# One offset for all tiles, half a projection moved to the last stage, and two pairs of banks swapped, in a two-layer encoder on one core

## The chip, the cores and the metric

The kernel runs on one core of a Trainium2 chip. The metric is the device time of one execution in microseconds (us); lower is better. TensorE (PE in the profile) multiplies, ScalarE (ACT) and VectorE (DVE) split, scale and add, SyncE (SP) issues the DMAs, GpSimd (POOL) does almost nothing.

## The reference

Two token sequences, 512 and 256 long, go through the same two layers with shared weights and a model width of 1024. Cut to what matters:

```python
for i in range(2):                      # layer 0: attention, layer 1: short convolution
    h = rms_norm(x, norm_mix[i])
    x = x + (window_attention(h, ...) if i == 0 else short_conv(h, ...))
    h = rms_norm(x, norm_mlp[i])
    x = x + square(relu(h @ mlp_w_up[i])) @ mlp_w_down[i]          # 1024 -> 4096 -> 1024
    gate = sigmoid(rms_norm(x, norm_ple[i]) @ ple_w_gate[i])
    x = x + (p[i] @ ple_w_proj[i]) * gate                          # p[i]: 256 inputs per token
return rms_norm(x, final_norm)
```

`p[i] @ ple_w_proj[i]`, the projected inputs, does not depend on x and can be made at any time.

## The kernel before, in words

**Precision.** Every float32 operand of a product is split in two parts of type fp32r: `hi`, a rounded copy that ACT makes, and `lo`, the rest, which DVE makes as operand minus `hi`. A product is then three matmuls: hi·hi, hi·lo, lo·hi.

**Stages.** The trace runs through: attention with its projections (0 to about 270 us); the first MLP (270 to 750), the gate with the projected inputs (750 to 860), the convolution mixer (860 to 1100), the second MLP (1100 to 1545), and the last stage (1545 to the end), which finishes the second MLP, makes the second gate and the final norm and stores both outputs. In the MLPs and the mixer most products go through a scheme with seven block products in place of eight: `seven_parts` and `down`, whose matmuls all stand on line 464 (`product7`). One such chunk is 84 matmuls of 384 columns: seven products of 12, into PSUM tiles named a, b, c, d (for `down`: a, b, B, C). Before a chunk's products, ACT and DVE form sums of weight blocks (`sum`) and split them into the weight tiles whi/wlo, zhi/zlo and vhi/vlo.

**Order.** In attention and in the last stage the instructions are first recorded as operations with a cost each and then laid out by a list scheduler (`Plan.order`); elsewhere the order is that of the code. Each engine works its own queue in that order.

**Places.** SBUF tiles come from pools, which are laid behind each other: `const`, `main` (x), `slots` (S0 to S31: activations and their parts), `wp` (raw weights and whi/wlo), `stat`, and then, for attention, `attn` and `tmpA`, and afterwards `more` (S32 and up, zhi/zlo, vhi/vlo, `sum`) and `tmpB`. Most tiles are a multiple of 512 bytes long in each partition, but a few are not: the tiles `z` and `y` of the mixer (771 floats in four of the places S), `fin` (16 floats in `stat`), and in `attn` the tiles rb, rc, mn, sm and L. Each of these shifts what is laid behind it. As built, byte addresses modulo 512 are: x 96; the places S 96, 128, 160, 192 and, for most, 224; whi/wlo and the raw weights 224; everything in `more` and `tmpB` 288; `attn` mostly 160, `tmpA` 160. A matmul therefore reads its weights (whi/wlo) at 224 or (zhi/zlo, vhi/vlo) at 288, and its moving operand at any of the six.

**Projected inputs of layer 1.** They are made early and kept in DRAM (`pj`, `pjt`) until the last stage loads them (tile `pr`). For the second sequence (256 tokens, two blocks of 128, kept with the tokens in the partitions) the first 512 of the 1024 features are made in attention (`second_projected`, line 1237, 12 matmuls of 512 columns) and the other 512 at the head of the first MLP (`second_inputs.product`, line 1388, called from `ahead`), together with half of the first sequence's.

**The head of the first MLP.** `ahead` makes six products, each in a PSUM bank of the pools A (4 banks), C (2) and B (2): `bank("AABBCC"[m], "pj")`. ACT copies each out (`copied`, line 1400), the last one only behind several steps of the norm. Then the first plain product `p` (line 1485) takes the four banks A, and the sums of squares of the norm (`ss`, line 238) take the two banks C.

**The last stage.** For the first sequence the gate is made in eight blocks m of features (`gates`). For the second sequence, `turn_over` transposes x (PE, tile `xt`) so that tokens stand in the partitions, and `gate_block(t, c)` makes the gate of token block t in three column blocks c of 384, 384 and 256 features (`BLOCK`), multiplies it with `pr`, adds it to x and squares; `finished(t, ...)` makes the final norm of the block and stores it.

Of the kernel before, what the change touches and what calls it, by code (L numbers as in the profile page):

```python
# [17 lines left out]
P = 128  # L18
# [32 lines left out]
def trunk_kernel(ctx: ExitStack, tc: tile.TileContext, a: dict, out: bass.AP):  # L51
# [413 lines left out]


    pj = [dram.tile([KB, P, n], F32, name=f"pj{l}") for l, n in enumerate((T, SEQS[0]))]
    pjt = dram.tile([SEQS[1] // P, P, D], F32, name="pjt")

    class Op:  # L470
        def __init__(self, engine, cost, run, after, behind, tail):
# [121 lines left out]
    def A(n):  # L593
        return 0.095 + 0.00084 * n

    def V(n):
        return 0.067 + 0.00104 * n
# [3 lines left out]
    def mixer_attention():  # L601
# [2 lines left out]
        psum = s1.enter_context(tc.tile_pool(name="psA", bufs=1, space=PSUM))  # L604
        ap = s1.enter_context(tc.tile_pool(name="attn", bufs=2))
        tmp = s1.enter_context(tc.tile_pool(name="tmpA", bufs=3))

        KHI, KLO, QS = (0, 1, 4, 8), (2, 3, 5, 9), (6, 7, 14, 15, 10, 11, 12, 13)
        PB = {"mm0": 1, "mm1": 1, "S": BS, "O": BO, "PT": BT}
# [126 lines left out]
        ET = mybir.EngineType  # L736
        wide = first(ones512, "DVE", 0.45, widen)

        rb = new("rb", 1, lambda: ap.tile([32, HEADS], F32, name="rb", bufs=1))
# [113 lines left out]
        HT = (("mm0", "mm1"), ("PT", "PT"), ("S", "S"))  # L853
        xs, acc, sqs = [], place(0, "acc", F32), []
        for m in range(KB):
            t = new("L", BL, lambda: ap.tile([P, 2 * LW], F32, tag="L", name="L", bufs=BL)[:, :T])
            projected(0, m, (wt, w1)[m // 4], part0, t, HT[m % 3], m in (2, 5))
            b, hi, lo = x[m // 2], place(16 + m, "xs_mix0"), place(24 + m, "xs_mix0")

            def xin(m=m, b=b):  # L860
                return b.t[:, m % 2, :]

            def high(m=m, hi=hi, xin=xin):
                act.activation(hi.t[:], xin(), AF.Copy, scale=gain(0, m))

            def low(m=m, hi=hi, lo=lo, xin=xin):
                dve.scalar_tensor_tensor(lo.t[:], xin(), gain(0, m), hi.t[:].bitcast(F32), ALU.mult, ALU.subtract)

            h = first(hi, "ACT", A(T) + 0.09, high, [x_in[m], vec_in], [b.key])
            l = first(lo, "DVE", V(T) + 0.06, low, [h], [b.key, hi.key])  # L870
            xs.append(block_of(hi, lo, [h, l]))
            if m == 0:
                added = first(acc, "ACT", A(T), lambda xin=xin: act.activation(acc.t[:], xin(), AF.Square), [x_in[m]], [b.key])
            else:
                sq = temp("n", "sq")
                s = first(sq, "ACT", A(T), lambda xin=xin, sq=sq: act.activation(sq.t[:], xin(), AF.Square), [x_in[m]], [b.key])
# [20 lines left out]
        for i, (ps, o, n, last) in enumerate(sso):  # L897
# [12 lines left out]
        rc = new("rc", 1, lambda: ap.tile([P, T // P], F32, name="rc", bufs=1))  # L910
        rt = bank("PT", "rt")

        def columns():
# [143 lines left out]
        def attend(g, n, lo_blk, hi_blk):  # L1057
# [3 lines left out]
            nk = k1 - k0 + 1  # L1061
            w = nk * P
            j0 = (k0 - n + 1) * P
            mn = new("mn", 2, lambda: ap.tile([P, REP], F32, name="mn"))
            sm = new("sm", 2, lambda: ap.tile([P, REP], F32, name="sm"))
            lg, sums = [], []
            for h in range(REP):
                hp, j = divmod(h, 2)
                H_ = REP * g + h
                if j == 0:  # L1070
                    L = new("L", BL, lambda: ap.tile([P, 2 * LW], F32, tag="L", name="L", bufs=BL).rearrange(
                        "p (a b) -> p a b", a=2))
# [130 lines left out]
        def second_projected():  # L1203
# [21 lines left out]
            w = prepared(fetched(a["proj"][1, 0]), 2)  # L1225
            for m in range(KB // 2):
                projected(1, m, w, part1, temp("n", "pjs"), ("mm0",), False)
            for i in range(SEQS[1] // P):
                b, prev, t = bank("mm1"), None, temp("n", "pjs")
                for k in range(2):  # L1230

                    def run(b=b, i=i, k=k):
                        o = W0 + i * P
                        wh, wl = w.parts[0][k], w.parts[1][k]
                        xh, xl = (p[:, o : o + P] for p in part1[k].parts())
                        for j, (a_, b_) in enumerate(((xh, wh), (xh, wl), (xl, wh))):
                            pe.matmul(b.t[:], lhsT=a_, rhs=b_, start=k == 0 and j == 0, stop=k == 1 and j == 2)

                    args = "PE", 3 * MM[512], run, [w.ready, part1[k].ready, prev], [*w.keys, *part1[k].keys]
                    prev = first(b, *args) if k == 0 else op(*args[:4], [b.key, *args[4]])  # L1240
# [116 lines left out]
    def second_inputs(places):  # L1357
# [35 lines left out]
    def ahead(norm, product, w, places):  # L1393
# [4 lines left out]
        def copied(m):  # L1398
            t = slot(places[m % len(places)], "pjs", F32)[:, :512]
            act.activation(t, ps[m][:], AF.Copy)  # L1400
# [358 lines left out]
    def last_stage(y1, y2, own, done, w0, norm, full, rest, prs, kept, accs):  # L1759
# [182 lines left out]
        for k in (2, 3, 4, 5, 6, 7, 0, 1):  # L1942
# [11 lines left out]
            for (hi, lo), to, src in ((most, slice(0, T), slice(0, T)), (less[i // 3], c, slice(T, D))):  # L1954
# [5 lines left out]
                    lo.t[:, to], raw.t[:, src], hi.t[:, to].bitcast(F32), ALU.subtract), [h], [raw.key, hi.key] + [lo.key] * again)  # L1960
                gw[k].append(pair_of(lambda hi=hi, lo=lo, to=to: (hi.t[:, to], lo.t[:, to]), [hi.key, lo.key], [h, l]))

        def weights(k, o, n):

            b, o = (gw[k][0], o) if o < T else (gw[k][1], o - T)
            return cut(b, slice(o, o + n))
# [60 lines left out]
        turned, roots = {}, []  # L2027

        def turn_over(t):
            for c, blk in enumerate(BLOCK):  # L2030
                ms = range(blk.start // P, blk.stop // P)
                b = ps("A", "xt")

                def run(b=b, ms=ms, c=c):
                    for i, m in enumerate(ms):
                        pe.transpose(b.t[:, i * P : (i + 1) * P], x(m, s0 + t * P, P), ident[:])
                    if c == 0:
                        pe.transpose(b.t[:, 3 * P : 3 * P + 1], r.t[0:1, s0 + t * P : s0 + (t + 1) * P], ident[0:1, 0:1])

                z = first(b, "PE", 0.11 * len(ms), run, [[xready[m][1] for m in ms], rstd if c == 0 else None], [r.key])  # L2040
                z.bonus = SOON
                n = len(ms) * P
                box = side if c == 2 else xt[t]
                e = (op if c else lambda *z: first(box, *z))(
                    "ACT", A(n), lambda b=b, c=c, n=n: act.activation(cols[t][c](), b.t[:, :n], AF.Copy),
                    [z], [b.key] + [box.key] * (c > 0))
                turned[t, c] = e
                if c == 0:
# [6 lines left out]
        def gate_block(t, c):  # L2055
            blk = BLOCK[c]
            n = blk.stop - blk.start
            box, xb = (side if c == 2 else xt[t]), cols[t][c]
            b = ps("CB"[c % 2], "gate")
            tok = slice(s0 + t * P, s0 + (t + 1) * P)  # L2060
            last = product(b, n, 3 * MM[n], [(cut(xs[k], tok), weights(k, blk.start, n)) for k in KO], prev=lasts[-1])
            lasts[-1] = last
            pr = loaded(lambda: pjt[t, :, blk], n)
            g = temp("t", "gt")
            u = sig = first(g, "ACT", A(n) + 0.09, lambda: act.activation(
                g.t[:, :n], b.t[:, :n], AF.Sigmoid, scale=small.t[:, t : t + 1]), [last, turned[t]], [b.key, small.key])
# [68 lines left out]
    def mixer_conv(norm, w, w1, early, nxt, wide, held, yplaces, hplaces, lplaces, behind):  # L2135
# [297 lines left out]
```

## Time and profile before

| | |
|---|---|
| median of 3 runs | 1657.99 us (1656.71 to 1659.47) |
| the profiled execution | 1659.18 us, of which its span is 1657.4 us |
| PE busy | 1637.0 us, 9371 matmuls |
| DVE busy | 1390.1 us |
| ACT busy | 921.8 us |
| DMA | 145.10 MB, mean 88 GB/s |
| granted TensorE clock | 0.999 |

The span runs from the first to the last instruction on the core; 1.78 us of the execution lie outside it. Matmuls overlap in time, so the duration that the profile gives for one is longer than the step from its start to the next one's start. The pace of PE is read from the starts.

### The profile page before, as it was taken

What the parts mean: (1) busy time and instruction counts of PE and PEld (TensorE: products, weight loads), DVE (VectorE), ACT (ScalarE), POOL (GpSimd) and SP (SyncE); (2) the same over time, 40 slices, a digit from 0 to 9 for tenths busy, and PEclk for the clock granted to TensorE, in tenths of its full rate; (3) what the DMA queues carried; (4) which work ended last, traced back from release to release, by engine and by line L of the source; (5) the groups of instructions that cost most, each with busy time, mean ns of one, the idle gap of its engine ahead of it and who ended that gap; (6) DMA issues with size and microseconds to landing.
All of it is one profiled execution on the core that took longest, in us unless ns stands there. A gap on an engine that the chain in (4) does not pass through costs nothing.

```text
span 1657.4 us, 24151 instructions
## 1 busy us (share of the span) xinstructions
PE 1637.0 (99%) x9371; PEld 1585.5 (96%) x9371; DVE 1390.1 (84%) x2209; ACT 921.8 (56%) x1458; POOL 11.7 (1%) x60
## 2 busy tenths in 40 slices
PE   9999999999999999999999999999999999999997
PEld 7888889999999999999999999999999999999987
DVE  7478897999899989977878887759989989998685
ACT  7378794755455445545654434555545545555455
POOL 0000000000000000000000000000000000000000
PEclk9999999999999999999999999999999999999999
DMA  8945423221222222132321222211212222212322
GB/s 274 225 117 136 95 62 96 90 76 65 68 73 77 65 76 77 64 95 77 112 73 52 77 67 76 78 61 52 77 64 77 74 68 77 77 64 77 100 95 99
DMA packets 48066, 145.10 MB, mean 88 GB/s; under 512 B 6176, under 2 KB 9632, under 8 KB 47952
## 3 DMA queue, kind: packets, MB, share of 16 engines
q1 hardware_dynamic: 47952, 143.57, 28.0%
q8 instruction: 73, 1.20, 0.3%
q14 instruction: 41, 0.34, 0.1%
HBM read 123.62 MB, written 10.49 MB: 81 GB/s over the span
## 4 chain that ended last, share of the span: by engine, by line
PE 88%; DVE 4%; DMA 4%; ACT 2%; issue 1%; SPq 0%; DVEq 0%; ACTq 0%
PE a L464 32%; PE b L464 8%; PE mm L132 8%; PE mm L677 5%; PE c L464 5%; PE d L464 5%; PE gate L132 4%; PE p L1485 4%; PE B L464 4%; PE C L464 4%; PE gate L1822 3%; PE down L1822 2%; PE O L1140 1%; PE pt L1125 1%; DMA wraw<-in_p 1%
## 5 line engine op out<-in xcount | busy, mean ns | idle before, releaser
L432 ACT ACTIVATE whi<-sum 128x1024 fp32r<-128x1024 f32 x66 | 70.2, 1063 | 259.3 <-PE a L464 230.0
L464 PE MATMUL a<-xs,whi 128*128 128x384 f32 x608 | 118.2, 336 | 0.6 <-DVE y L1603 0.6
L464 PE MATMUL a<-t,zhi 128*128 128x384 f32 x528 | 108.1, 337 | 0.0
L464 PE MATMUL b<-t,zhi 128*128 128x384 f32 x528 | 108.0, 337 | 0.0
L464 PEld LDWEIGHTS a<-xs,whi 128*128 128x128 f32 x608 | 106.4, 188 | 1.5 <-DVE y L1603 1.2
L464 PE MATMUL a<-t,whi 128*128 128x384 f32 x528 | 107.6, 336 | 0.0
L1644 DVE TENSOR_TENSOR x<-x,a 128x384 f32<-128x384 f32 x112 | 62.1, 555 | 53.2 <-PE a L464 53.0
L464 PE MATMUL a<-act,whi 128*128 128x384 f32 x448 | 96.0, 335 | 0.0
L464 PEld LDWEIGHTS b<-t,zhi 128*128 128x128 f32 x528 | 94.0, 188 | 0.0
L464 PEld LDWEIGHTS a<-t,zhi 128*128 128x128 f32 x528 | 93.8, 188 | 0.0
L464 PEld LDWEIGHTS a<-t,whi 128*128 128x128 f32 x528 | 93.4, 188 | 0.0
L432 ACT ACTIVATE zhi<-sum 128x1024 fp32r<-128x1024 f32 x66 | 69.8, 1058 | 36.1 <-DVE sum L408 30.3
L443 DVE TENSOR_TENSOR wlo<-wraw,whi 128x1024 fp32r<-128x1024 f32 x72 | 87.8, 1219 | 0.0
L432 ACT ACTIVATE whi<-wraw 128x1024 fp32r<-128x1024 f32 x72 | 75.7, 1051 | 19.3 <-issue 15.7
L677 PE MATMUL mm<-xs_mix,whi 128*128 128x512 f32 (+1 forms) x320 | 80.8, 339 | 0.3 <-DVE vv L1028 0.3
L443 DVE TENSOR_TENSOR zlo<-sum,zhi 128x1024 fp32r<-128x1024 f32 x66 | 80.4, 1218 | 0.6 <-ACT zhi L432 0.6
L443 DVE TENSOR_TENSOR wlo<-sum,whi 128x1024 fp32r<-128x1024 f32 x66 | 80.5, 1220 | 0.0
L464 PEld LDWEIGHTS a<-act,whi 128*128 128x128 f32 x448 | 79.4, 188 | 0.0
L464 PE MATMUL a<-xs,wlo 128*128 128x384 f32 x304 | 65.6, 337 | 0.0
L464 PE MATMUL b<-t,zlo 128*128 128x384 f32 x264 | 61.5, 337 | 0.7 <-DVE zlo L443 0.7
L464 PE MATMUL a<-t,zlo 128*128 128x384 f32 x264 | 61.6, 337 | 0.0
L464 PE MATMUL a<-t,wlo 128*128 128x384 f32 x264 | 61.0, 335 | 0.0
(384 smaller groups left out, 4488.5 us busy)
## 6 DMA issues: line engine op xcount, KB each, us to landing
wraw<-in_up SPq DMA_DIRECT2D x64, 512.0 KB, 3.4
wraw<-in_down SPq DMA_DIRECT2D x64, 512.0 KB, 3.5
wraw<-in_w_in SPq DMA_DIRECT2D x24, 512.0 KB, 3.4
wraw<-in_gate SPq DMA_DIRECT2D x16, 512.0 KB, 3.5
wraw<-in_w_q SPq DMA_DIRECT2D x8, 512.0 KB, 5.5
wraw<-in_w_out SPq DMA_DIRECT2D x8, 512.0 KB, 3.5
x_in<-in_x SPq DMA_DIRECT2D x8, 384.0 KB, 7.2
pj<-L SPq DMA_DIRECT2D x8, 384.0 KB, 4.9
```

The lines of the kernel that those rows point to most:

```text
L132: pe.matmul(t, lhsT=w, rhs=x[:, o:e], start=first and i == 0 and j == 0, stop=last and i == n - 1 and j == 2)
L432: act.activation(hi[:], src, AF.Copy)
L443: dve.tensor_tensor(lo[:], src, hi[:].bitcast(F32), ALU.subtract)
L464: pe.matmul(ps, lhsT=a, rhs=b, start=start and i == 0, stop=i == len(terms) - 1, skip_group_check=True)
L677: pe.matmul(ps.t[:, :n], lhsT=a_, rhs=b_, start=k == 0 and j == 0, stop=k == len(xs) - 1 and j == 2,)
L1125: pe.transpose(pt.t[:, h * P : (h + 1) * P], lg[h // 2].t[:, h % 2, 1 + b * P : 1 + (b + 1) * P], ident[:],)
L1140: pe.matmul(O.t[:], lhsT=vb, rhs=part.t[:], start=b == 0 and i == 0, stop=b == nk - 1 and i == 1)
L1485: pe.matmul(ps[i][o], lhsT=wt[:, c], rhs=xs[f"x{h + 1}{1 + o}"][m][part], start=k == 0 and j == 0, stop=k == KB - 1 and j == 2,)
L1644: dve.tensor_tensor(t[:, o : o + H], t[:, o : o + H], f, op)
L1822: pe.matmul(ps.t[:, o : o + n], lhsT=a_, rhs=b_, start=begin and i == 0 and j == 0, stop=end and i == len(terms) - 1 and j == 2,)
```

## The change: what it does

It has four parts.

1. **Offsets.** The tiles of odd length in `attn` move to a pool `odd` that is laid behind the others; the mixer's z and y are allocated 896 floats long and cut to 771; `fin` moves from `stat` to `tmp`, behind `more`. As built, every tile of main, slots, wp, stat, attn, tmpA, more and tmpB then lies at 96 modulo 512. All matmuls of 384 and more columns read both operands at 96, but for those that read the constant `ones`.
2. **Projected inputs.** The products at line 1237 and their copies and stores go out of attention; `pjt` holds 512 features only. The last stage loads the second sequence's 256 inputs (128x2x256) and a projection weight tile (128x1024), splits them into vhi/vlo and zhi/zlo, and `gate_block(t, 0)` makes the product (6 matmuls of 512 columns, tile `pj`, a bank A) and multiplies with it straight from its bank, without a DRAM round trip.
3. **Column blocks.** `BLOCK` becomes 512, 256 and 256 features. `turn_over` takes the blocks in the order 1, 0, 2, and the column of the norm's factor rides with block 1.
4. **Banks of the head.** `"AABBCC"` becomes `"AACCBB"`.

```diff
-    pjt = dram.tile([SEQS[1] // P, P, D], F32, name="pjt")
+    pjt = dram.tile([SEQS[1] // P, P, D // 2], F32, name="pjt")
...
+        odd = s1.enter_context(tc.tile_pool(name="odd", bufs=2))
...
-            t = new("L", BL, lambda: ap.tile([P, 2 * LW], F32, tag="L", name="L", bufs=BL)[:, :T])
+            t = new("L", BL, lambda: odd.tile([P, 2 * LW], F32, tag="L", name="L", bufs=BL)[:, :T])
...
             for m in range(KB // 2):
                 projected(1, m, w, part1, temp("n", "pjs"), ("mm0",), False)
-            for i in range(SEQS[1] // P):
-                b, prev, t = bank("mm1"), None, temp("n", "pjs")
-                for k in range(2):
...
-                e = first(t, "ACT", A(512), lambda b=b, t=t: act.activation(t.t[:, :512], b.t[:], AF.Copy), [prev], [b.key])
-                dma(None, lambda i=i, t=t: (pjt[i, :, :512], t.t[:, :512]), 262144, [e], [t.key])
...
-            ps = bank("AABBCC"[m], "pj")
+            ps = bank("AACCBB"[m], "pj")
...
-            nc.sync.dma_start(pj[1][h + m] if m < h else pjt[m - h, :, 512:], t)
+            nc.sync.dma_start(pj[1][h + m] if m < h else pjt[m - h], t)
...
-        BLOCK = slice(0, 3 * P), slice(3 * P, 6 * P), slice(6 * P, D)
+        BLOCK = slice(0, 4 * P), slice(4 * P, 6 * P), slice(6 * P, D)
...
+        raw = new("wraw", 3, lambda: wp.tile([P, CH], F32, name="wraw", bufs=3))
+        raw.ready = [dma(raw, lambda raw=raw: (raw.t[:, : 2 * s1].rearrange("p (k n) -> p k n", k=2), a["p"][1, :, :, s0:]), 8 * P * s1)]
+        inputs2 = []
+        for i, (names, n) in enumerate(((("vhi", "vlo"), 2 * s1), (("zhi", "zlo"), CH))):
+            if i:
+                raw = fetched(a["proj"][1, 0])
+            hi, lo = (new(t, 1, lambda t=t, n=n: more.tile([P, n], F32R, tag=t, name=t, bufs=1)) for t in names)
+            h = first(hi, "ACT", A(n), lambda hi=hi, raw=raw, n=n: act.activation(hi.t[:], raw.t[:, :n], AF.Copy), [raw.ready], [raw.key])
+            l = first(lo, "DVE", V(n), lambda hi=hi, lo=lo, raw=raw, n=n: dve.tensor_tensor(
+                lo.t[:], raw.t[:, :n], hi.t[:].bitcast(F32), ALU.subtract), [h], [raw.key, hi.key])
...
-        small = new("fin", 1, lambda: stat.tile([P, 16], F32, tag="fin", name="fin"))
+        small = new("fin", 1, lambda: tmp.tile([P, 16], F32, tag="fin", name="fin", bufs=1))
...
-            for c, blk in enumerate(BLOCK):
+            for c in (1, 0, 2):
+                blk = BLOCK[c]
...
+            if c == 0:
+                pr = ps("A", "pj")
+                pr.ready = [product(pr, n, 3 * MM[n], [(cut(inputs2[0][k], slice(t * P, t * P + P)), inputs2[1][k]) for k in range(2)], prev=lasts[-1])]
+                lasts[-1] = pr.ready[0]
+            else:
+                pr = loaded(lambda: pjt[t, :, blk.start - D // 2 : blk.stop - D // 2], n)
...
-        zs, ts = ([slot(i, name, F32, Z) for i in ps] for name, ps in (("z", wide[:2]), ("y", wide[2:])))
+        zs, ts = ([slot(i, name, F32, T + P)[:, :Z] for i in ps] for name, ps in (("z", wide[:2]), ("y", wide[2:])))
```

What the scheduler makes of it is seen at three places. The first is PE in attention, where the first of the four groups of removed matmuls stood. `O` is the attention's weighted sum, `mm<-whi,p` the removed product, `mm<-xs_mix` a query product, `pt` transposes the softmax, `S` are scores. Before:

```order
L1140 MATMUL O<-pl,vv 128x512
L1237 MATMUL mm<-whi,p_728 128x512
L1237 MATMUL mm<-wlo,p_728 128x512
L1237 MATMUL mm<-whi,p_736 128x512
L677 MATMUL mm<-xs_mix_186,whi 128x512
L677 MATMUL mm<-xs_mix_199,whi 128x512
L677 MATMUL mm<-xs_mix_186,wlo 128x512
L1125 MATMUL pt<-ident,L 128x128 x8
```

After:

```order
L1141 MATMUL O<-pl,vv 128x512
L1126 MATMUL pt<-ident,L 128x128 x8
L1083 MATMUL S<-kk,q 128x256
L1084 MATMUL S<-kk,q 128x256
L1083 MATMUL S<-kk,q 128x256
L1084 MATMUL S<-kk,q 128x256
L678 MATMUL mm<-xs_mix_189,whi 128x512
L678 MATMUL mm<-xs_mix_202,whi 128x512
```

The transposes and the next scores move forward by the three removed matmuls and by three query matmuls, which now come behind them.

The second is DVE in the last stage, where the factor of the second gate's norm (`rstd_ple`) is made and the first gate blocks use it (`gt<-gate`). Before:

```order
L1911 TENSOR_SCALAR v<-ss 128x256
L1928 SCALAR_TENSOR_TENSOR v<-ln,v 128x768
L1930 SCALAR_TENSOR_TENSOR rstd_ple_15746<-v,y 128x768
L1994 TENSOR_TENSOR gt<-gate,rstd_ple_15746 128x512 x3
L1997 TENSOR_TENSOR gt<-pr,gt 128x512 x2
```

After:

```order
L1897 TENSOR_SCALAR v<-ss 128x256
L1914 SCALAR_TENSOR_TENSOR v<-ln,v 128x768
L1957 TENSOR_TENSOR zlo<-wraw,zhi 128x1024
L1916 SCALAR_TENSOR_TENSOR rstd_ple_15747<-v,y 128x768
L1957 TENSOR_TENSOR vlo<-wraw,vhi 128x512
L1993 TENSOR_TENSOR gt<-gate,rstd_ple_15747 128x512 x3
L1996 TENSOR_TENSOR gt<-pr,gt 128x512 x2
```

The two new subtractions stand on either side of the norm's last step, ahead of the first use.

The third is PE in the last stage at the change from the first block of 128 tokens to the second. In the changed kernel the rows are:

```order
L1808 MATMUL gate<-whi,xs_ple_15361 128x256
L1808 MATMUL gate<-wlo,xs_ple_15361 128x256
L1808 MATMUL gate<-whi,xs_ple_15371 128x256
L1808 MATMUL pj<-zhi,vhi 128x512
L1808 MATMUL pj<-zlo,vhi 128x512
L1808 MATMUL pj<-zhi,vlo 128x512
L1808 MATMUL pj<-zhi,vhi 128x512
L1808 MATMUL pj<-zlo,vhi 128x512
L1808 MATMUL pj<-zhi,vlo 128x512
```

Six `pj` matmuls stand between the two blocks, where before the next block's gate followed at once; six more stand ahead of the first block.

More of the change, by code (lines that the diff above doesn't have):

```diff
@@ L737, in mixer_attention @@
         wide = first(ones512, "DVE", 0.45, widen)
-        rb = new("rb", 1, lambda: ap.tile([32, HEADS], F32, name="rb", bufs=1))
+        rb = new("rb", 1, lambda: odd.tile([32, HEADS], F32, name="rb", bufs=1))
         oh = new("bias", 4, lambda: ap.tile([32, 512], F32, tag="bias", name="oh", bufs=4))
@@ L909, in mixer_attention @@
             r.t[:], v.t[:], 1.5, y.t[:], ALU.add, ALU.mult), [newton], [v.key, y.key])
-        rc = new("rc", 1, lambda: ap.tile([P, T // P], F32, name="rc", bufs=1))
+        rc = new("rc", 1, lambda: odd.tile([P, T // P], F32, name="rc", bufs=1))
         rt = bank("PT", "rt")
@@ L1063, in attend @@
             j0 = (k0 - n + 1) * P
-            mn = new("mn", 2, lambda: ap.tile([P, REP], F32, name="mn"))
-            sm = new("sm", 2, lambda: ap.tile([P, REP], F32, name="sm"))
+            mn = new("mn", 2, lambda: odd.tile([P, REP], F32, name="mn"))
+            sm = new("sm", 2, lambda: odd.tile([P, REP], F32, name="sm"))
             lg, sums = [], []
@@ L1070, in attend @@
                 if j == 0:
-                    L = new("L", BL, lambda: ap.tile([P, 2 * LW], F32, tag="L", name="L", bufs=BL).rearrange(
+                    L = new("L", BL, lambda: odd.tile([P, 2 * LW], F32, tag="L", name="L", bufs=BL).rearrange(
                         "p (a b) -> p a b", a=2))
@@ L1227, in second_projected @@
                 projected(1, m, w, part1, temp("n", "pjs"), ("mm0",), False)
-            for i in range(SEQS[1] // P):
-                b, prev, t = bank("mm1"), None, temp("n", "pjs")
-                for k in range(2):
[L1232 to L1240, printed above, removed]
-                e = first(t, "ACT", A(512), lambda b=b, t=t: act.activation(t.t[:, :512], b.t[:], AF.Copy), [prev], [b.key])
-                dma(None, lambda i=i, t=t: (pjt[i, :, :512], t.t[:, :512]), 262144, [e], [t.key])
         load_bias(0)
@@ L1961, in last_stage @@
                 gw[k].append(pair_of(lambda hi=hi, lo=lo, to=to: (hi.t[:, to], lo.t[:, to]), [hi.key, lo.key], [h, l]))
+        raw = new("wraw", 3, lambda: wp.tile([P, CH], F32, name="wraw", bufs=3))
[8 more added lines that the diff above has]
+                lo.t[:], raw.t[:, :n], hi.t[:].bitcast(F32), ALU.subtract), [h], [raw.key, hi.key])
+            wide2 = pair_of(lambda hi=hi, lo=lo: (hi.t, lo.t), [hi.key, lo.key], [h, l])
+            inputs2.append([cut(wide2, slice(k * n // 2, (k + 1) * n // 2)) for k in range(2)])
         def weights(k, o, n):
@@ L2036, in run @@
                         pe.transpose(b.t[:, i * P : (i + 1) * P], x(m, s0 + t * P, P), ident[:])
-                    if c == 0:
+                    if c == 1:
                         pe.transpose(b.t[:, 3 * P : 3 * P + 1], r.t[0:1, s0 + t * P : s0 + (t + 1) * P], ident[0:1, 0:1])
-                z = first(b, "PE", 0.11 * len(ms), run, [[xready[m][1] for m in ms], rstd if c == 0 else None], [r.key])
+                z = first(b, "PE", 0.11 * len(ms), run, [[xready[m][1] for m in ms], rstd if c == 1 else None], [r.key])
                 z.bonus = SOON
@@ L2043, in turn_over @@
                 box = side if c == 2 else xt[t]
-                e = (op if c else lambda *z: first(box, *z))(
+                again = box.op is not None
+                e = (op if again else lambda *z: first(box, *z))(
                     "ACT", A(n), lambda b=b, c=c, n=n: act.activation(cols[t][c](), b.t[:, :n], AF.Copy),
-                    [z], [b.key] + [box.key] * (c > 0))
+                    [z], [b.key] + [box.key] * again)
                 turned[t, c] = e
-                if c == 0:
+                if c == 1:
                     f = first if t == 0 else lambda _, *z: op(*z)
```

3 lines of the change are left out of this document (1 added, 2 removed).

## The prediction

> **What bounds the kernel now.** I read the page first: the busy times and the shares of the chain that ended last.
>
> ```profile
> span 1657.4 us, 24151 instructions
> PE 1637.0 (99%) x9371; PEld 1585.5 (96%) x9371; DVE 1390.1 (84%) x2209; ACT 921.8 (56%) x1458; POOL 11.7 (1%) x60
> PE 88%; DVE 4%; DMA 4%; ACT 2%; issue 1%; SPq 0%; DVEq 0%; ACTq 0%
> ```
>
> PE is busy all the way and carries 88% of the chain. A change can shorten the run in two ways only: fewer or quicker matmuls, or less of the 20.4 us in which PE stands still (1657.4 - 1637.0). Where those are, the stages tell (columns: length, then busy time and count of PE, PEld, DVE, ACT and, where it has any, POOL; then the granted clock, the DMA share and GB/s):
>
> ```profile
> 100.00:160.00 60.00, 59.94 (x371) 52.23 (x370) 54.90 (x160) 55.41 (x141) 4.07 (x22) 1.00 0.55 150
> 160.00:180.00 20.00, 16.72 (x93) 14.18 (x92) 11.75 (x33) 9.09 (x23) 1.31 (x2) 1.00 0.70 143
> 180.00:272.00 92.00, 91.29 (x559) 80.63 (x558) 82.65 (x209) 72.39 (x169) 4.40 (x19) 1.00 0.31 87
> 272.00:1147.00 875.00, 872.57 (x4978) 868.92 (x4977) 744.14 (x1067) 461.96 (x634) 0.33 (x6) 1.00 0.23 73
> 1147.00:1570.00 423.00, 422.63 (x2424) 419.25 (x2423) 379.73 (x544) 223.06 (x327) 0.00 (x0) 1.00 0.23 75
> ```
>
> From 272 to 1570 us PE stands still for 2.43 + 0.37 = 2.8 us in 1298. There the order of instructions is the same before and after; only addresses and the banks of the head change. So what the change does there is the pace of 7402 matmuls, and one stall. The clock is 1.00 throughout and plays no part.
>
> **Part 1, the offsets.** Pace is read from starts. This is PE in one chunk of seven products, each of 12 matmuls, in the first MLP (start, duration, operation):
>
> ```profile
> 440.24 1.55 PE L464 MATMUL a<-xs,whi 128*128 128x384 f32 x8
> ...
> 442.32 1.56 PE L464 MATMUL b<-t,zhi 128*128 128x384 f32 x8
> ...
> 444.42 1.58 PE L464 MATMUL a<-t,zhi 128*128 128x384 f32 x8
> ...
> 446.54 1.54 PE L464 MATMUL c<-xs,whi 128*128 128x384 f32 x8
> ...
> 448.63 1.58 PE L464 MATMUL a<-t,whi 128*128 128x384 f32 x8
> ...
> 450.76 1.56 PE L464 MATMUL d<-t,vhi 128*128 128x384 f32 x8
> ...
> 452.85 1.55 PE L464 MATMUL a<-xs,whi 128*128 128x384 f32 x8
> ...
> 454.94 1.54 PE L464 MATMUL a<-xs,whi 128*128 128x384 f32 x8
> ```
>
> The starts are 2.08, 2.10, 2.12, 2.09, 2.13, 2.09 and 2.09 us apart, 14.70 together, or 175.0 ns for each of 84 matmuls. Against the quickest, 2.08, the products lose 0.00, 0.02, 0.04, 0.01, 0.05, 0.01 and 0.01: 0.14 a chunk. How many chunks there are, the splits of the weight tile vhi tell, one for each chunk (the ACT column, x66):
>
> ```profile
> 272.00:1600.00 1328.00, 107.72 (x528) 93.65 (x528) 45.25 (x66) 40.85 (x66) 1.00 0.23 74
> ```
>
> If every product ran at 2.08, 66 x 0.14 = 9.2 us would go: the most that this part can bring by these rows. What is sure to change is the products whose weights lie at 288 modulo 512 while nearly everything else lies at 224: b and a with zhi, d with vhi. They lose 0.02 + 0.04 + 0.01 = 0.07, so 66 x 0.07 = 4.6 us. The product a with whi loses most, 0.05, though its weights and most of its moving tiles are already at one offset; that speaks for something else behind it, and I leave it as it is. The 0.01 of d is as small as the rows can be read, so I count the zhi products alone: 66 x 0.06 = **-4.0 us**. That I take equal offsets to be the cause is a choice: the xs tiles lie at several offsets against whi at 224 and run at 2.08 to 2.09 all the same. From the other side the bound is a pace at which more products run like a with whi: seven at 2.13 make 14.91, 0.21 above 14.70, so 66 x 0.21 = 13.9 us more; I keep half, +7, as this term's upper end, since that one product shows that a common offset of operands does not forbid the slow pace.
>
> [...]
>
> **Part 4, the banks of the head.** Here is the one large stall after attention, and the first DVE step that could use the time (the bracket is the idle time before it and what ended it):
>
> ```profile
> 304.85 0.34 PE L238 MATMUL ss<-al,ones 128*128 128x384 f32 x1
> 305.81 0.58 ACT L1400 ACTIVATE pjs<-pj 128x512 f32<-128x512 f32 x1
> 306.44 0.44 PE L238 MATMUL ss<-ah,ones 128*128 128x384 f32 x1 [1.25 <-ACT pjs L1400]
> 312.17 1.23 DVE L443 TENSOR_TENSOR zlo<-wraw,zhi 128x1024 fp32r<-128x1024 f32 x1 [0.71 <-ACT zhi L432]
> ```
>
> The second `ss` needs the bank C that the last early product still holds until its copy at 305.81. PE goes 1.59 us from start to start where the pace is 0.17: 1.42 us lost. With the late products in the banks B, which nothing needs until the second chunk, the wait goes. What is late next is DVE, which stands at 0.71 idle before zlo and then works through to these two waits of PE:
>
> ```profile
> PE a L464 <- DVE y L1603: 0.4, 1, 0.4
> PE b L464 <- DVE zlo L443: 0.4, 1, 0.4
> ```
>
> If DVE can pull forward only its 0.71, the gain is 0.7; if it keeps up, 1.4. I take **-1.0**.
>
> **Part 2, the projection moved.** Twelve matmuls of 512 columns leave attention and twelve come into the last stage. Their step and the stage they leave:
>
> ```profile
> 119.69 0.39 PE L1237 MATMUL mm<-whi,p 128*128 128x512 f32 x1
> 119.92 0.39 PE L1237 MATMUL mm<-wlo,p 128*128 128x512 f32 x1
> ...
> PE S L1082 <- DMA q<-ql: 3.3, 2, 2.3
> ...
> 162.29 0.39 PE L1082 MATMUL S<-kk,q 128*128 128x256 f32 x1 [0.94 <-DMA q<-ql]
> ...
> 175.66 0.35 PE L1082 MATMUL S<-kk,q 128*128 128x256 f32 x1 [2.35 <-DMA q<-ql]
> ...
> 200.00:240.00 40.00, 39.90 (x246) 34.77 (x245) 39.27 (x114) 34.83 (x91) 2.59 (x12) 1.00 0.33 87
> ```
>
> The step is 0.23 us, so 12 x 0.23 = 2.76 us of PE leave, and 2.76 come back in the last stage, where PE is full and nothing hides them. The two copies and two stores (one ACT and one SP instruction each) leave as well; SP's queue is then shorter for the loads of the keys and queries. Does attention give its 2.76 back? From 100 to 160 PE is full, so the work behind moves forward. Against it stand two things. The two waits for q (0.94 and 2.35) end with a load that follows its own product on PE; as the product moves with the rest, the waits stay about as long. And from 200 to 240 DVE is busy 39.27 of 40: there PE cannot go faster than DVE. DVE did have 5.1 us idle from 100 to 160 and 8.3 from 160 to 180, so most of its work can move along. I take 2.0 of the 2.76 as given back: **+0.8**. All of it gives 0, none +2.8.
>
> In the last stage the two splits come on ACT and DVE. They don't appear there before; the same shapes elsewhere do, and the place where DVE meets them:
>
> ```profile
> 341.63 0.61 ACT L432 ACTIVATE vhi<-wraw 128x512 fp32r<-128x512 f32 x1
> 343.55 0.69 DVE L443 TENSOR_TENSOR vlo<-wraw,vhi 128x512 fp32r<-128x512 f32 x1
> ...
> 1597.78 0.96 DVE L1930 SCALAR_TENSOR_TENSOR rstd_ple<-v,y 128x768 f32<-128x768 f32 x1
> 1599.54 1.89 DVE L1994 TENSOR_TENSOR gt<-gate,rstd_ple 128x512 f32<-128x512 f32 x3 [0.80 <-PE gate L1822]
> ```
>
> On DVE, zlo (1.23) and vlo (0.69) are 1.92 us around the norm's last step, and 0.80 is idle there: the first gate blocks come some 1.1 us later. What hides this is the banks: PE needs the next gate bank only after several products more, so I cost it at nothing; if that cover is gone, PE waits up to 1.1 us once. ACT gains 0.61 and 1.06 and loses two copies of 0.58; it is busy 56% of the span. SP gets two more loads, at the head of the stage, long before their use.
>
> **Part 3 and the tail.** The total of columns stays 1024. The tail before:
>
> ```profile
> 1646.74 1.02 DVE L2067 TENSOR_TENSOR gt<-pr,gt 128x384 f32<-128x384 f32 x2
> ...
> 1648.13 0.28 PE L1822 MATMUL gate<-whi,xs_ple 128*128 128x256 f32 x1
> 1648.27 0.52 ACT L2071 ACTIVATE gt<-xt 128x384 f32<-128x384 f32 x1 [1.57 <-DVE xt L2069]
> 1649.29 0.46 ACT L2065 ACTIVATE gt<-gate,fin 128x256 f32<-128x256 f32 x1
> ...
> 1654.18 0.38 SPq L1789 DMA_DIRECT2D out<-xt  x1
> ```
>
> PE's last matmul ends at 1648.41, but the sigmoid of that gate starts at 1649.29: 0.88 us behind two squares on ACT, which wait for DVE (1.57). Afterwards the first sequence's final norm, whose scaling kept DVE behind, lies further ahead of PE's end, by the products that now stand between, and the blocks before the last are done earlier. So up to 0.88 goes; I take **-0.7**. A chain as long as before gives 0.
>
> **Sum.** -4.0 - 1.0 + 0.8 - 0.7 = -4.9 us. The profiled execution took 1659.18, so 1654.3. It lies 1.19 above the median of the three runs (1657.99, between 1656.71 and 1659.47); against the median the forecast is **1653.1 us**. By the ends: -9.2 - 1.4 + 0 - 0.9 = -11.5, and +7 - 0.7 + 2.8 + 0 = +9.1.
>
> **The rivals.**
>
> *The offsets do nothing.* Then -1.0 + 0.8 - 0.7 = -0.9 remains: 1657.1, no change. For it: the xs products, whose offsets differ, run at 2.08 to 2.09, and the slowest product, a with whi, has mostly equal offsets. Against it: zhi and whi products of one shape differ by up to 0.04 in 2.08 in the chunk shown, and something in the places must make that. [...]
>
> *All products run at the quick pace.* The a with whi product is slow only by those of its tiles that lie elsewhere (some are at 96 and 160), and its 0.05 goes with the rest: -9.2 - 0.9 = -10.1, so 1647.9, faster.
>
> *One offset makes the two streams of PE collide (slower).* Weights are loaded while the matmul before reads its moving operand; PEld is busy 96% of the span. If reads at one offset modulo 512 meet in the same place, products with unequal offsets lose what they had. For it: a with whi, at one offset, is the slowest of seven. Half the worst, +7, and -0.9: +6.1, so 1664.1. It decides from where the chunk's pace passes 175.0 ns by more than 0.6 (66 x 84 x 0.0006 = 3.3 us), that is 14.75 a chunk. Against it: the last product of the chunk, also at 224 in most of its tiles, runs at 2.09.
>
> *The move costs its matmuls twice.* Attention is held by DVE and gives nothing back, the last stage pays 2.76, and the sigmoid stays late: +2.8 - 1.0 + 0, and the offsets' -4.0, make -2.2: 1655.8, within the noise.
>
> *The change isn't what it says* can be left out for the order, which shows the products moved; for the offsets, it would be the first rival.
>
> **How the numbers follow.** Some 0.2%, 3.3 us, is what a measurement of this kernel can tell from no change: faster is below 1654.7, slower above 1661.3. The forecast has a chance of 0.45; its own terms can take it past 1654.7 in about 0.08 of that. The rivals: offsets do nothing 0.20, all quick 0.15, collision 0.12, the move given nothing back 0.08. Faster: 0.45 - 0.08 + 0.15 + 0.02 of the move's = 0.54. Slower: 0.12 and 0.02 from the first rival with the move at its dearest, 0.14. The rest, 0.32, is no change. The range goes from just under all quick, 1647.5, up to 1662, which holds all cases but the third rival, and leaves out the collision and the far end below.
>
> **What would show it.** In the changed profile: product starts in a chunk of the first MLP with b and a of zhi at 2.08 (right), all at 2.08 (second rival) or several at 2.13 and above (collision); the stretch 272 to 1570 shorter by about 5; the 1.25 wait of `ss` gone and the waits for y and zlo longer; the seam at 272 some 2 us earlier; the last sigmoid right behind PE's last matmul. The forecast is wrong if the chunk's pace stays at 175.0 ns or rises.

## The result, and the profile after

The changed kernel takes 1647.92 us (median of 4 runs, 1647.24 to 1648.74) against 1657.61 us for the kernel before (4 runs). The ratio is 0.994 with a 95% interval of 0.9923 to 0.9958, so it is faster by 0.4 to 0.8%. Later rounds gave 1647.67 and a ratio of 0.9941 (0.9929 to 0.9953).

The first lines of its page, as those shown of before:

```profile
span 1646.9 us, 24149 instructions
PE 1628.5 (99%) x9371; PEld 1574.8 (96%) x9371; DVE 1389.6 (84%) x2211; ACT 920.1 (56%) x1458; POOL 10.2 (1%) x60
PE 88%; DVE 5%; DMA 5%; ACT 2%; issue 1%; SPq 0%; DVEq 0%; ACTq 0%
```

PE has the same 9371 matmuls and is still 99% busy, but for 8.5 us less. The span is 10.5 us shorter, so PE's standing still shrank by only 2 us. Most of the gain is pace. The timeline of PE for the chunk that the prediction showed (start, duration, operation) says the same:

```profile
436.38 1.55 PE L464 MATMUL a<-xs,whi 128*128 128x384 f32 x8
...
438.46 1.55 PE L464 MATMUL b<-t,zhi 128*128 128x384 f32 x8
...
440.54 1.55 PE L464 MATMUL a<-t,zhi 128*128 128x384 f32 x8
...
442.62 1.55 PE L464 MATMUL c<-xs,whi 128*128 128x384 f32 x8
...
444.70 1.55 PE L464 MATMUL a<-t,whi 128*128 128x384 f32 x8
...
446.78 1.55 PE L464 MATMUL d<-t,vhi 128*128 128x384 f32 x8
...
448.86 1.55 PE L464 MATMUL a<-xs,whi 128*128 128x384 f32 x8
...
450.94 1.55 PE L464 MATMUL a<-xs,whi 128*128 128x384 f32 x8
```

All seven products are 2.08 us apart, 14.56 together, 173.3 ns for a matmul. Those that were at 2.10 to 2.13 before have come down, the product a with whi among them.

To see where the time went, I cut the span at starts in PE's timeline: the first `pj` matmul of the first MLP's head, the first `down` matmul of the last stage, PE's last matmul, and the end. In these marks the profiled runs read (us; the first four columns are stretches, the last is the span):

```
                     to pj   pj to down   down to last   last to end     span
before               292.33     1251.90         103.90          9.26   1657.4
after                290.19     1242.74         105.73          8.28   1646.9
offsets alone        289.88     1243.75         103.07          9.22   1645.9
banks alone          291.76     1251.00         103.92          9.25   1655.9
move and blocks      289.72     1252.06         106.59          8.27   1656.6
offsets and banks    291.93     1242.72         103.10          9.21   1647.0
 ... and blocks      291.00     1242.71         103.05         10.06   1646.8
after, again         289.16     1242.72         105.74          8.28   1645.9
```

From before to after: -2.14, -9.16, +1.83, -0.98, together -10.45. The second column repeats to 0.03 us among the four rows that have both the offsets and the banks. The first doesn't: among the five rows with the projection still in attention it goes from 289.88 to 292.33, so single differences there of 1 or 2 us prove nothing.

### The profile page after: what moved, and what is told of

It is laid out like the page before. It is cut to its first block, busy times and chain, and to the rows that moved or that the text cites. A ratio compares the mean times of both kernels' runs of the same rounds, so it can differ in the third digit from the quotient of the medians.

```text
span 1646.9 us, 24149 instructions
## 1 busy us (share of the span) xinstructions
PE 1628.5 (99%) x9371; PEld 1574.8 (96%) x9371; DVE 1389.6 (84%) x2211; ACT 920.1 (56%) x1458; POOL 10.2 (1%) x60
## 4 chain that ended last, share of the span: by engine, by line
PE 88%; DVE 5%; DMA 5%; ACT 2%; issue 1%; SPq 0%; DVEq 0%; ACTq 0%
PE a L464 32%; PE b L464 8%; PE mm L132 8%; PE d L464 5%; PE c L464 5%; PE mm L678 4%; PE p L1471 4%; PE gate L132 4%; PE gate L1808 4%; PE B L464 4%; PE C L464 4%; PE down L1808 2%; DMA q<-ql 2%; PE O L1141 1%; PE pt L1126 1%; DMA skew<-brow 1%
```

## The experiments

### The parts by themselves

**Offsets alone.** The kernel before with part 1 of the change:

```diff
+        odd = s1.enter_context(tc.tile_pool(name="odd", bufs=2))
-        rb = new("rb", 1, lambda: ap.tile([32, HEADS], F32, name="rb", bufs=1))
+        rb = new("rb", 1, lambda: odd.tile([32, HEADS], F32, name="rb", bufs=1))
...
-        small = new("fin", 1, lambda: stat.tile([P, 16], F32, tag="fin", name="fin"))
+        small = new("fin", 1, lambda: tmp.tile([P, 16], F32, tag="fin", name="fin", bufs=1))
-        zs, ts = ([slot(i, name, F32, Z) for i in ps] for name, ps in (("z", wide[:2]), ("y", wide[2:])))
+        zs, ts = ([slot(i, name, F32, T + P)[:, :Z] for i in ps] for name, ps in (("z", wide[:2]), ("y", wide[2:])))
```

Expected:

> Part 1 alone, on the kernel before: only the addresses change. Theory (the offsets carry the gain): all products of 384 columns at 173.3 ns from start to start, 14.56 us a chunk instead of 14.70, and the run 9 us shorter, about 1648.5, a ratio of 0.9945; the two stalls of 1.42 and 0.54 us at the head of the first MLP stay as they are. Rival (the offsets work only together with the other parts, or the gain lies in the order of attention and the last stage): a pace of 174 to 175 ns and less than 4 us.

Measured: 1648.03 us, ratio 0.9931 (0.9919 to 0.9944). This part alone makes the whole gain, within the uncertainty. In the table it takes 8.15 us from the middle and 0.83 from the last stage. The other 2.45 us of its shorter span lie ahead of pj, in the column that scatters: the row "offsets and banks", with the same attention, has 291.93 there. The rival falls.

**Banks alone.** `"AABBCC"` to `"AACCBB"` in the kernel before.

> Part 4 alone, on the kernel before. Theory (the stall of 1.42 us goes, and half of it comes back as a longer wait for the convolved tile y in front of the second chunk, which grows from 0.54 to 1.25 us): -0.7 us, a ratio of 0.9996, nothing that the rounds can tell from 1. Rival (DVE keeps up, the whole stall goes): -1.4 us, a ratio of 0.9991.

Measured: 1657.55 us, ratio 0.9992 (0.9983 to 1.0001), not told from no change by the time. The profile tells more: the middle is 0.90 us shorter, and the waits of PE there are one fewer, with the one for `y` grown from 0.4:

```profile
PE a L464 <- DVE y L1603: 0.9, 1, 0.9
...
PE b L464 <- DVE zlo L443: 0.4, 1, 0.4
```

The wait for the bank is gone, and a part of it has become a wait for DVE. In the changed kernel that wait is 1.1:

```profile
PE a L464 <- DVE y L1589: 1.1, 1, 1.1
...
PE b L464 <- DVE zlo L443: 0.4, 1, 0.4
```

**Move and column blocks alone.** The changed kernel with its offsets and its head banks as before.

```diff
-            ps = bank("AACCBB"[m], "pj")
+            ps = bank("AABBCC"[m], "pj")
-        small = new("fin", 1, lambda: tmp.tile([P, 16], F32, tag="fin", name="fin", bufs=1))
+        small = new("fin", 1, lambda: stat.tile([P, 16], F32, tag="fin", name="fin"))
...
```

> Parts 2 and 3 alone, on the kernel before: offsets and head banks as before. Theory: attention ends 2.0 us earlier, the last stage gets 2.8 us more, and the tail from PE's last matmul to the end is 1.0 us shorter: -0.2 us, a ratio of 0.9999. Rival (attention is held by DVE and the loads of q and gives nothing back): +1.8 us, a ratio of 1.0011.

Measured: 1658.42 us, ratio 0.9999 (0.999 to 1.0007). The terms are all there and cancel: the last stage is 2.69 us longer, the tail 0.99 shorter, and the stretch to pj 2.61 shorter, though that column scatters by as much.

### What it is about the offsets

**Pairs of offsets, by themselves.** A kernel of its own with nothing but matmuls.

```diff
+EQUAL = [(o, o) for o in (0, 32, 64, 96, 128, 160, 224, 256, 288, 352, 416, 480)]
+APART = [(96, o) for o in (64, 128, 160, 224, 288, 352, 416, 480)] + [(288, 224), (224, 288)]
+            w0, m0 = ws[i % len(ws)] // 4 + 128 * k, ms[i % len(ms)] // 4 + 768 * m
+            pe.matmul(b[:, :N], lhsT=wts[:, w0 : w0 + P], rhs=mov[:, m0 : m0 + N], ...)
```

> A kernel of its own that leaves out the whole computation: it writes zeros and runs groups of 48 matmuls of 384 columns, with nothing beside them, each group with its weights at one byte offset modulo 512 and its moving operand at one. Twelve groups have equal offsets, from 0 to 480; ten have unequal ones; four change the offset of one or both from matmul to matmul. Theory (unequal offsets of the two operands cost time): equal groups 173.3 ns at every offset, unequal ones 174 to 177. First rival (a change of offset from one matmul to the next costs it, not the pair): groups with constant offsets 173.3, equal or not, and only the four changing ones slower. Second rival (96 itself is the good place): 173.3 at 96, more at 224 and 288 even with equal offsets. Third rival (what costs is traffic of other engines or DMA that meets PE at unequal offsets): 173.3 in all groups.

Measured, from the starts: groups with equal offsets settle to 173.3 ns at all twelve offsets tried, so 96 is no better than another. Three of them in PE's timeline (`w96m` has its weights at 96; the trace drops the last digits of the names). Their starts are 8.34 to 8.35 us apart for 48 matmuls, at one offset as at the other:

```profile
53.04 8.51 PE L49 MATMUL w64m<-mov,wts 128*128 128x384 f32 x48
61.39 8.51 PE L49 MATMUL w96m<-mov,wts 128*128 128x384 f32 x48
69.73 8.51 PE L49 MATMUL w128m<-mov,wts 128*128 128x384 f32 x48
```

Call the moving operand's offset less the weights' offset the distance. At distances of 32, 128 and 192 bytes the pace settles to 176.7, 176.0 and 174.7; at 384 it is 176.0 and at -64 174.7, like 128 and 192. At -32, 64, 256 and 320 it is 173.3 to 173.5. So it isn't equality that counts. In eleven of the twelve equal groups, each of which follows one at another offset, the first six steps are about 173, 175, 177, 185, 176 and 182 before the pace settles: 28 ns lost in the change. (The first of the twelve lost only 3.) The groups whose offsets change at every matmul ran at 175.0 to 176.5. The first theory and the first rival were each half right, and the other two fell.

**A chunk replayed at its addresses, and the distance in steps of 32 bytes.**

```diff
+RUNS = [("before", BEFORE), ("after", AFTER),
+    ("zeven", [(w - 64 if w % 512 == 288 else w, m) for w, m in BEFORE]),
+    ("meven", [(w, at(m, 224)) for w, m in BEFORE]),
+    ("one288", [(at(w, 288), at(m, 288)) for w, m in BEFORE]),
+    ("plus64", [(w, m + 64) for w, m in AFTER]), ("minus64", [(w + 64, m) for w, m in AFTER]),
+    ("zplus256", ...), ("zplus128", ...)]
...
+            group("d" + "abcdefghijklmnop"[d // 32], [(2048 + 512 * (i % 8) + 96, 8192 + 3072 * (i % 16) + 96 + d) for i in range(96)])
```

> A kernel of its own that leaves out the whole computation and replays one chunk of 84 matmuls at its SBUF addresses (all shifted by 7 x 4096 bytes), four times over, with zeros as data and nothing beside it; then sixteen groups of 96 matmuls whose moving operand lies 0, 32, ... 480 bytes further modulo 512 than the weights. Theory (PE's own two reads collide, by their distance modulo 256 and by changes of it; no other engine has a part in it): the chunk of the kernel before at 14.70 us as in the full run, that of the changed kernel at 14.56; with the moving operand 64 bytes behind the weights everywhere 14.56, with it 64 bytes ahead 14.67 (84 x 174.7); with the weights of b, the zhi product of a and d moved by 256 bytes 14.56, by 128 more than 14.60. Groups at distances d and d + 256 have one pace. First rival (other engines' or DMA traffic causes it): 14.56 for both replays. Second rival (modulo 512 counts): the 256-byte case is slower, and d and d + 256 differ.

The timeline of PE in this run; one row is one group, with its first start. The trace drops digits from names: `one` is one288, and the row `zplus` holds both zplus groups; `da` to `dp` are the distances 0 to 480:

```profile
53.43 58.97 PE L92 MATMUL before<-big 128*128 128x384 f32 x336
112.23 58.41 PE L92 MATMUL after<-big 128*128 128x384 f32 x336
170.48 58.89 PE L92 MATMUL zeven<-big 128*128 128x384 f32 x336
229.21 58.89 PE L92 MATMUL meven<-big 128*128 128x384 f32 x336
287.93 58.43 PE L92 MATMUL one<-big 128*128 128x384 f32 x336
346.20 58.41 PE L92 MATMUL plus<-big 128*128 128x384 f32 x336
404.45 59.51 PE L92 MATMUL minus<-big 128*128 128x384 f32 x336
463.80 117.04 PE L92 MATMUL zplus<-big 128*128 128x384 f32 x672
...
595.24 16.80 PE L92 MATMUL da<-big 128*128 128x384 f32 x96
611.88 16.80 PE L92 MATMUL db<-big 128*128 128x384 f32 x96
628.52 16.80 PE L92 MATMUL dc<-big 128*128 128x384 f32 x96
645.16 17.12 PE L92 MATMUL dd<-big 128*128 128x384 f32 x96
662.12 17.06 PE L92 MATMUL de<-big 128*128 128x384 f32 x96
679.01 16.82 PE L92 MATMUL df<-big 128*128 128x384 f32 x96
695.66 16.93 PE L92 MATMUL dg<-big 128*128 128x384 f32 x96
712.43 16.81 PE L92 MATMUL dh<-big 128*128 128x384 f32 x96
729.09 16.83 PE L92 MATMUL di<-big 128*128 128x384 f32 x96
745.75 16.80 PE L92 MATMUL dj<-big 128*128 128x384 f32 x96
762.39 16.80 PE L92 MATMUL dk<-big 128*128 128x384 f32 x96
779.03 17.12 PE L92 MATMUL dl<-big 128*128 128x384 f32 x96
795.99 17.06 PE L92 MATMUL dm<-big 128*128 128x384 f32 x96
812.89 16.81 PE L92 MATMUL dn<-big 128*128 128x384 f32 x96
829.54 16.93 PE L92 MATMUL do<-big 128*128 128x384 f32 x96
846.31 16.82 PE L92 MATMUL dp<-big 128*128 128x384 f32 x96
```

From start to start, the chunk of before takes 58.80 / 4 = 14.70 us and that of after 58.25 / 4 = 14.56: what the chunk shown takes in the full kernels, with no other engine at work and some 1 GB/s of DMA on the page. Even the single products come out alike (2.08, 2.09, 2.12, 2.09, 2.13, 2.09, 2.09 for before). So the addresses that PE reads, and nothing else, make the 0.14. With zhi and vhi alone brought to 224 a chunk is 14.68; with the moving tiles alone at 224 it is 14.68; with all at 288 it is 14.57 with the change from the group before. A distance of 64 everywhere costs nothing (14.56), of -64 0.28 (14.84, more than I expected). That is 176.7 ns a matmul, where the groups at one constant distance of -64 or 192 ran at 174.7. The price of a distance was not the same in both, and no run shows by itself what makes the difference. By the single starts zplus256 takes 14.56 and zplus128 14.66, as expected. The distances: 96, 128 and 192 bytes cost (16.96, 16.89 and 16.77 us for 96 matmuls against 16.64), and 352, 384 and 448 take just as long; the others, 32 and 64 among them, do not. So the distance counts modulo 256. That 32 bytes is free here (16.64) and was not in the run before (176.7 ns a matmul against 173.3) stays unexplained: the order of the weight blocks and the high address bits differ between the two, and neither was tried by itself.

**The same in the whole kernel.** The changed kernel with unused bytes ahead of the pool `more`, 256, 128 or 64:

```diff
+    ctx.enter_context(tc.tile_pool(name="pad", bufs=1)).tile([P, 64], F32, name="pad")
     more = ctx.enter_context(tc.tile_pool(name="more", bufs=1))
```

> The changed kernel with 256 unused bytes ahead of the pool more: zhi, vhi, their lo parts and the places from S32 on lie at 352 modulo 512, the rest at 96. Theory (modulo 256): as the changed kernel, 1648, and every product at 173.3 ns. Rival (modulo 512, one offset for all is what is needed): pairs at unequal offsets in most products, as in the kernel before: 1653 to 1658.

> The same with 128 unused bytes: more lies at 224, the rest at 96. Theory (modulo 256): unequal pairs lie 128 bytes apart, which the first probe ran at 176.1 ns in place of 173.3; with about half of the 7400 matmuls of the middle in such pairs 3700 x 2.7 ns = +10 us over the changed kernel, about 1658, and some more or less by the changes between pairs. Rival (what counts is something else that the change did): 1648.

> The same with 64 unused bytes: more lies at 160, the rest at 96. Theory (the pair and its sign count): the zhi, vhi products on tiles at 96 have the moving operand 64 bytes ahead of the weights, 174.7 ns in the first probe; the whi products on tiles at 160 have it 64 behind, 173.3 ns: some 66 x 30 x 1.4 ns = +2.8 us, with changes of pairs up to +6: 1650 to 1654, between the two others. Rival (any unequal offset costs the same): as with 128 bytes.

Measured: 1648.71 us with 256 bytes (0.994, 0.9927 to 0.9954), as fast as the changed kernel though two offsets modulo 512 meet in most products; 1658.82 with 128 (1.0004, 0.9995 to 1.0013), all of the gain gone; 1656.78 with 64 (0.9994, 0.9985 to 1.0002). The stretch from pj to down takes 1242.79, 1252.76 and 1250.46 us. Modulo 256 is shown. The last case came out worse than expected: 64 bytes cost 7.7 us there where I had 2.8 to 6. I had priced the distance of -64 by the first probe, 1.4 ns a matmul; by the replay it is 3.3 (0.28 / 84), and 66 x 30 x 3.3 = 6.5 us, an estimate that would explain most of it. The rival, the same cost as with 128 bytes, is 2.3 us off in this stretch. The 128-byte chunk in PE's timeline, its first and last product and the start of the next chunk:

```profile
437.03 1.57 PE L464 MATMUL a<-xs,whi 128*128 128x384 f32 x8
...
449.67 1.57 PE L464 MATMUL a<-xs,whi 128*128 128x384 f32 x8
...
451.77 1.57 PE L464 MATMUL a<-xs,whi 128*128 128x384 f32 x8
```

14.74 us, 0.18 above the changed kernel, and 66 x 0.18 = 11.9 is near the 10.0 that the middle lost.

### Is there a quicker one?

**Offsets and banks, without the move; and the same with the new column blocks.** Parts 1 and 4, then parts 1, 3 and 4, on the kernel before, beside the changed kernel again:

```diff
-        BLOCK = slice(0, 3 * P), slice(3 * P, 6 * P), slice(6 * P, D)
+        BLOCK = slice(0, 4 * P), slice(4 * P, 6 * P), slice(6 * P, D)
-            for c, blk in enumerate(BLOCK):
+            for c in (1, 0, 2):
+                blk = BLOCK[c]
```

> Parts 1 and 4 without the moved projection and the new column blocks. From the runs so far: offsets alone -10.4, banks -0.9 in the profile's head, and the matmuls of the projection stay in attention, where with the offsets made equal they seemed to cost nothing: 1647, within a microsecond of the whole change. Rival (the move pays once the offsets are equal): 1649 or more.

> Parts 1, 3 and 4 without the moved projection. If the shorter tail (1.0 us less from PE's last matmul to the end) comes from the column blocks alone, it is there without the move as well: 1646, the quickest so far. Rival (it comes from the six products that now stand between the two token blocks): the tail is as long as before, and the time as without the blocks.

> The changed kernel once more, on the chip of the two others: 1648, for the comparison. If the two others are quicker, the move of the projection is what costs them nothing and this one a microsecond or two.

Measured: 1646.68, 1647.89 and 1647.67 us, ratios 0.9935 (0.9921 to 0.9948), 0.9941 (0.9929 to 0.9954) and 0.9941 (0.9929 to 0.9953). The three can't be told apart, so none of them beats the changed kernel clearly. The blocks alone do not shorten the tail: it is 10.06 us, against 9.21 without them. It is short only in the kernels that have the six products between the token blocks.

## Why the prediction was right or wrong

The forecast was 1653.1, faster; the result is 1647.92, faster. The direction held, and so did the cause, unequal offsets; which products they slow was wrong, and that term was half of what it is. The result lies 0.4 us above the lower end of the range (1647.5), where the second rival had put it: the range held narrowly, and not by the path that the forecast took.

**Offsets: forecast -4.0, measured -8.15 in the middle and -0.83 in the last stage.** This is the mis-sized term. The step that failed is "I count the zhi products alone", with the product a with whi left as it is because "its weights and most of its moving tiles are already at one offset". Two things were missing in it. First, two of that product's eight moving tiles lie, by the addresses as built, at 96 and 160, which is 128 and 192 modulo 256 from weights at 224: costly distances (176.0 and 174.7 ns a matmul against 173.3 in the first probe), and offsets that changed at every matmul ran at 175.0 to 176.5 there. Second, the xs tiles that the first product reads lie at 288 against weights at 224, at 64, one of the free distances (16.64 us for 96 matmuls in the replay, as at 0). So their pace of 2.08 was no evidence that offsets don't matter. In the replay the step as I had it, zhi and vhi moved to 224 and nothing else, gives 0.02 a chunk: 66 x 0.02 = 1.3 us, less still than the 4.0; with that size the sum would have been -2.2 us, which the prediction counted as no change, so its own path did not lead to "faster", and that the direction came out right owes something to luck. With all operands alike the whole 0.14 goes (14.57 with all at 288), and this was the second rival, all products at 2.08; it gave 1647.9.

The bound of 9.2 from the chunk's rows held (8.15 measured in the middle). By their starts the 66 chunks together went from 971.6 us to 964.0 with the offsets alone, so 7.6 of the 8.15 is theirs. The collision rival had a true core: the pace does depend on where the two operands lie to each other, but equal offsets are a free case (173.3 ns at all twelve offsets of the first probe; -64 everywhere made the replayed chunk 14.84 in place of 14.56). One argument against it in the prediction was misread: in the last product of the chunk, which ran at 2.09, six of the eight moving tiles lie at 288 by the replayed addresses and only two at 224, so most of it has the free distance 64 and not equal offsets. The first rival, that the offsets do nothing, doesn't agree with the replay: 14.70 against 14.56 with PE alone at work.

**Banks: forecast -1.0; measured -0.9 alone and -1.03 on top of the offsets** (1243.75 to 1242.72). DVE was late next, as foreseen: the wait for y is 1.1 now.

**The move: forecast +0.8.** In the last stage it costs 2.69 (forecast 2.76). In attention the six profiled runs with the move reach the first pj 289.06 to 290.20 us into the span, the five without it 289.88 to 292.33; the means, 289.74 and 291.38, are 1.6 apart, where I had 2.0. So about +1.0, as far as these runs can tell. The waits for q stayed, as foreseen: 2.5 us in three here, 3.3 in two before, and between 1.9 and 3.5 over all the profiled runs, with the move or without:

```profile
PE S L1083 <- DMA q<-ql: 2.5, 3, 2.1
```

The splits on DVE were hidden, as costed: in the changed kernel's timeline zlo and vlo stand around the norm's last step, the first gate block follows without idle time, and no wait of PE is listed from 1560 us on:

```profile
1586.04 1.23 DVE L1957 TENSOR_TENSOR zlo<-wraw,zhi 128x1024 fp32r<-128x1024 f32 x1
1587.18 0.95 DVE L1916 SCALAR_TENSOR_TENSOR rstd_ple<-v,y 128x768 f32<-128x768 f32 x1
1588.05 0.69 DVE L1957 TENSOR_TENSOR vlo<-wraw,vhi 128x512 fp32r<-128x512 f32 x1
1588.65 1.88 DVE L1993 TENSOR_TENSOR gt<-gate,rstd_ple 128x512 f32<-128x512 f32 x3
```

**Tail: forecast -0.7, measured -0.98.** The timeline of the last gate, its sigmoid and the last store:

```profile
1638.66 0.28 PE L1808 MATMUL gate<-whi,xs_ple 128*128 128x256 f32 x1
...
1638.98 0.47 ACT L2071 ACTIVATE gt<-gate,fin 128x256 f32<-128x256 f32 x1 [0.23 <-PE gate L1808]
...
1643.72 0.38 SPq L1775 DMA_DIRECT2D out<-side  x1
```

The sigmoid waits for PE alone now and starts at 1638.98, 0.04 us after that matmul's end, where it stood 0.88 behind before.

The move and the tail together come to nothing (+1.0 - 1.0), as their own run says with 0.9999. The whole change is the offsets, plus a microsecond from the banks.

## What to carry to other kernels

In a kernel that PE bounds, look at the steps between starts of equal matmuls in one stretch; where they differ from product to product, compare the SBUF addresses of weights and moving operand before looking for waits (here the same chunk took 14.70 us at the addresses of before and 14.56 at those of after, with PE alone at work). Size such a term by all products that are above the quickest, not by those that one guess at the cause covers, and replay one stretch at its real addresses: that settled here in one run what the rows of the trace could not. A short odd tile in a pool shifts all that is laid behind it: here 64 bytes ahead of `more` moved it from 96 to 160 modulo 512.

## What the runs showed of the hardware

With no other engine at work, the pace of TensorE depended on where the weights and the moving operand lay relative to each other. For 384 columns of fp32r in steps of 173.3 ns, the groups behind the replay lost 3.3 ns a matmul, once settled, at a distance of 96 bytes, 2.6 at 128 and 1.4 at 192, modulo 256, and nothing at the others. A whole chunk at -64, which is 192 modulo 256, lost 3.3. A change of offsets cost up to 28 ns over six matmuls in the first probe before the pace settled. Why it is these distances, why 32 cost in one probe (176.7 ns a matmul) and not in the other (16.64 us for 96), and why -64 cost 3.3 ns in a chunk and 1.4 in a group, is open. What inside PE or SBUF makes the loss, no run shows.
